# A float32 two-block network on one core: masks of the second block moved from TensorE to VectorE, tanh gates, and lighter VectorE work in the first block

## The chip, the cores and the metric

The kernel runs on one core of one Trainium2 chip. The metric is the device time of one execution in microseconds (us), a median over runs. The engines are named PE (TensorE), DVE (VectorE), ACT (ScalarE), POOL (GpSimd) and SP (SyncE, which here only starts transfers).

## The reference, cut to what matters

The first block is one layer: a projection into queries, keys, values, a convolution branch and a recurrent branch; three patterns of windowed attention; an output projection; a feed-forward part. The second block has two layers of latent attention (8 heads, 1040 tokens of which 16 are added in front) beside a pooling branch, each branch under a sigmoid gate.

```python
def conv_module(a, gate, dw_w, dw_b, ln_g, ln_b):
    u = a * jax.nn.sigmoid(gate)
    u = causal_depthwise_conv(u, dw_w, dw_b)            # 31 taps
    return jax.nn.silu(layernorm(u, ln_g, ln_b))
...
    u = causal_depthwise_conv(xr, cw, cb)               # 4 taps, then rg_lru
...
# second block, each of two layers
    y_pool = (pool_mix(u_pool, ...) * jax.nn.silu(z_pool)) @ pool_w_up[l]
    o_mla = mla(...)      # per head: softmax(mask(q k^T * scale)) v, causal
    y_mla = (o_mla * jax.nn.silu(z_mla)) @ mla_w_up[l]
    merged = jax.nn.sigmoid(g_pool) * y_pool + jax.nn.sigmoid(g_mla) * y_mla
    h_res = h_res + merged @ w_out[l]
```

## The kernel before

Channels lie on the partitions and tokens along the free axis. Every large product is made of three matmuls on a high and a low part of each operand (`mm3`, L125 to L127: high weight by high activation, high by low, low by high). `w()` (L109 to L119) brings a weight tile by a transfer that SP starts, copies its high part on ACT (L117) and makes the low part on DVE (L118). Results leave PSUM in 512-column pieces, or in pieces of 344 and 352 for the 1040 tokens. PSUM is split into 5 buffers with the tag mm and 3 with the tag ax. In SBUF there are pools u (30 tiles of a row block), s (10) and d (6). The engines run their instructions in a fixed order each; the framework sets that order when the kernel is built, from the order in which the code writes the work and from the priorities that it is given.

**First block.** While the projections into q, k and v run on PE, a list of background generators is stepped after every 512-column piece, by `pump` at the rate `RATE1` (60 before: 6.0 us of estimated DVE work to a piece). The generators are `conv_bg` (31 taps for each of two channel tiles, L429), `ln_bg` (layer norm after the convolution, L448 to L480) and three `lru_bg` (L486 to L526). `colsum` (L230) sums over partitions by matmuls against a column of ones, and `bcast` (L248) spreads the result. What is left of the background is run out by `hook` before attention starts. The drains of the projection are L396 (lx, lg) and L772 (q, k, v) on DVE.

**Second block.** `attn2` goes through the heads in steps (key tile j, query piece). `s_part` issues three matmuls into `st` (L1592 to L1594) and, where the step touches the diagonal, a fourth that adds the mask out of an identity times a mask table in bfloat16 (L1596). `evac` then takes the exponential on ACT (L1602), the high part `ph` on ACT or DVE (L1605, L1607) and the low part `pl` on DVE (L1608). `o_part` multiplies by the values (L1624 to L1626) three steps later (`LAG=3`). Between these matmuls stand those of the next head's preparation: `fp` (L1535) spreads norm factors over rows, `mx` (L1552, with the mask added in L1554) makes the scores once more to find each query's maximum (L1555 on DVE). Also between them stand the units of `fill`: the gate projections first, then the up-projection of the pooling branch (`mm<-th`), whose operand is read back from DRAM (`tr`, L1270 to L1273). `run` keeps back `keep` units of fill for the end of the last head: 2 for each of its columns before. After the last head the softmax sums go over DRAM (`rh`, L1473) and are spread by `rb` (L1490) before the up-projection of attention (`mm<-oh`) starts. The gates are taken by a sigmoid on ACT at L1282 (pooling) and L1407 (attention).

`fp` contracts over 57 rows (high part in rows 0 to 24, low part from row 32), `rb` over 40 (low part from row 32).

Of the kernel before, what the change touches and what calls it, by code (L numbers as in the profile page):

```python
# [11 lines left out]
F32R = mybir.dt.float32r  # L12
# [6 lines left out]
P = 128  # L19
# [27 lines left out]
def f(t):  # L47
    return t.bitcast(F32)


class B:
# [175 lines left out]
    def colsum(self, acc, tiles, nrows=P, pin=False):  # L227
        ps = self.axb("cs")
        for j, (c0, n) in enumerate(tiles):
            ins = self.nc.tensor.matmul(ps[:n, j:j + 1], acc[:nrows, c0:c0 + n], self.ones[:nrows, :], start=True, stop=True)  # L230
            if pin and j == 0:
                self.tc.keep_in_program_order(ins)
# [72 lines left out]
    def _block1(self):  # L305
# [140 lines left out]
        def ln_bg():  # L446
            sm = self.u("sm")
# [5 lines left out]
            mub = self.u("mub")  # L453
# [3 lines left out]
            q0, q1 = self.u("q"), self.u("q")  # L457
# [12 lines left out]
            rb = self.u("rb")  # L470
# [3 lines left out]
            for ct in range(2):  # L474
                a = cv[ct]
                nc.vector.tensor_tensor(a[:, :S], a[:, :S], rb[:, :S], op=OP.mult)
                sg = self.u("sg")
                nc.scalar.activation(sg[:, :S], a[:, :S], AF.Sigmoid, scale=col("lng", ct), bias=col("lnb", ct))
                nc.vector.tensor_scalar(a[:, :S], a[:, :S], col("lng", ct), col("lnb", ct), op0=OP.mult, op1=OP.add)
# [4 lines left out]
        def lru_bg(i):  # L484
            uu = self.u("uu")
            nc.vector.tensor_scalar(uu[:, :S], lx[i][:, :S], col("lw", 9 + i), col("lb", i), op0=OP.mult, op1=OP.add)  # L486
            yield 1.2
# [5 lines left out]
            r, ig = self.u("r"), self.u("ig")  # L493
# [36 lines left out]
        lx, lg = [], []  # L530
        for i in range(3):
# [8 lines left out]
            self.bg.append(lru_bg(i))  # L540
# [29 lines left out]
        def hook(stp):  # L570
            if stp == (0, 0, 0):
                self.flush()
                self.rate = 0
            if stp == (1, 0, 0):
                mix_in(5)
                mix_in(6)
                mix_in(7)
# [106 lines left out]
    def attn1(self, xh, xl, wk, win, scaled, hook):  # L684
# [7 lines left out]
        for hh in range(2):  # L692
            nc.vector.tensor_copy(bm[:, 3 * hh:3 * hh + 3, :], bmf[hh][:, :768].rearrange("p (a b) -> p a b", a=3))
# [127 lines left out]
        def s_part(g, j, b):  # L821
# [240 lines left out]
    def layer(self, l):  # L1062
# [190 lines left out]
        def fill():  # L1253
# [14 lines left out]
            for g in range(4):  # L1268
# [3 lines left out]
                nc.vector.tensor_copy(h[:, M0:], t[:, M0:])  # L1272
                nc.vector.tensor_tensor(lo[:, M0:], t[:, M0:], f(h[:, M0:]), op=OP.subtract)  # L1273
                th.append(h)
                tl.append(lo)
            for m in range(8):
# [5 lines left out]
                nc.scalar.activation(t[:, M0:], t[:, M0:], AF.Sigmoid)  # L1282
                y = mp[m] = self.u("mp")
                for c0, n in CM:
                    ps = self.mmb()
                    for k in range(4):
# [3 lines left out]
                        if k == 3:  # L1290
                            nc.vector.tensor_tensor(y[:, c0:c0 + n], ps[:, :n], t[:, c0:c0 + n], op=OP.mult)
# [32 lines left out]
        fr = self.ur("frh", (57, L2))  # L1324
        nc.gpsimd.memset(f(fr[0:57, :]), 0.0)

        def qstats():
# [8 lines left out]
            for g in range(3):  # L1336
# [7 lines left out]
                nc.vector.tensor_tensor(fr[32:57, c0:c0 + wd], ps[0:25, :wd], f(fr[0:25, c0:c0 + wd]), op=OP.subtract)  # L1344
# [56 lines left out]
        for m in range(8):  # L1401
# [5 lines left out]
            nc.scalar.activation(t[:, M0:], t[:, M0:], AF.Sigmoid)  # L1407
# [5 lines left out]
            def ev(ci, c0, n, ps, t=t, y=y, h=h, lo=lo):  # L1413
                nc.vector.tensor_tensor(t[:, c0:c0 + n], ps, t[:, c0:c0 + n], op=OP.mult)
# [44 lines left out]
    def rlgrp(self, l, h0, h1):  # L1459
# [11 lines left out]
        for q, t in ((0, rlh), (32, rll)):  # L1471
# [27 lines left out]
    def attn2(self, l, fr, fill):  # L1499
# [10 lines left out]
        self.rh = self.ur("rh", (40, L2))  # L1510
        nc.gpsimd.memset(f(self.rh[0:40, :]), 0.0)
# [394 lines left out]
```

## Time and profile before

| what | value |
|---|---|
| median of 3 runs | 2974.47 us (2971.53 to 2975.08) |
| the profiled execution's own time | 2971.57 us |
| its span | 2969.8 us |
| PE busy | 2893.7 us (97%) |
| DVE busy | 1707.3 us (57%) |
| ACT busy | 973.8 us (33%) |
| POOL busy | 33.7 us (1%) |
| mean granted TensorE clock | 0.984 |

Busy time is the time in which at least one instruction of an engine is under way. Matmuls overlap: a row of 512 columns is shown with 0.39 us, but such rows start 0.23 us apart. So a busy PE can still be a PE that does less than it could, and the distance from one start to the next is what a matmul costs. The chain of waits follows the work that ended last back from the end. A number in brackets behind a row of the timeline is the idle time just before the instruction, with the instruction or transfer that ended it.

### The profile page before, as it was taken

Reading aid. Unit: us, or ns where it says so; the run is one execution under the profiler, and the core shown is the slowest. Engines: PE = TensorE matmul, PEld = TensorE weight load, DVE = VectorE, ACT = ScalarE, POOL = GpSimd, SP = SyncE. Lnnn points to the kernel's source line nnn. Section 1 sums busy time; section 2 is a strip of 40 time slices with the busy share of each in tenths; the row PEclk is TensorE's granted clock in tenths of the full one; section 3 lists DMA queues with packets and bytes.
Section 4 is the critical chain, followed back from the end, with each engine's and each line's share of the span. In section 5 each row is a group of like instructions: output and inputs, shape, how many; then the busy total and the mean of one; then the engine's idle time right before and its main releaser. Section 6 shows DMA issues by size and latency. Waiting matters only on the chain.

```text
span 2969.8 us, 37159 instructions
## 1 busy us (share of the span) xinstructions
PE 2893.7 (97%) x14918; PEld 2442.2 (82%) x14918; DVE 1707.3 (57%) x2940; ACT 973.8 (33%) x1617; POOL 33.7 (1%) x101
## 2 busy tenths in 40 slices
PE   8979999999999999999999999989999999999999
PEld 6857788888888888899899998879978887777677
DVE  6986766544545546544665665564534665656562
ACT  4143432111111124433234343743432223433630
POOL 1000000000000000000000000000000000000000
PEclk9989999999999999999999999989999999999999
DMA  3111212111111111524223232532313323232542
GB/s 129 54 36 64 86 59 69 46 50 50 43 50 50 43 47 53 174 62 125 65 83 91 76 101 59 187 112 105 123 54 98 116 75 91 88 85 74 177 141 76
DMA packets 93520, 249.93 MB, mean 84 GB/s; under 512 B 29489, under 2 KB 30786, under 8 KB 93348
## 3 DMA queue, kind: packets, MB, share of 16 engines
q1 hardware_dynamic: 93348, 247.56, 26.3%
q8 instruction: 117, 1.92, 0.3%
q14 instruction: 55, 0.45, 0.0%
HBM read 182.86 MB, written 60.06 MB: 82 GB/s over the span
## 4 chain that ended last, share of the span: by engine, by line
PE 93%; DVE 4%; ACT 1%; DMA 1%; issue 0%; SPq 0%; POOL 0%; DVEq 0%; ACTq 0%; POOLq 0%
PE mm L125 27%; PE mm L127 26%; PE mm L126 26%; PE mx L1552 1%; PE st L1593 1%; PE st L1594 1%; PE st L1592 1%; PE ob L1624 1%; PE ob L1626 1%; PE ob L1625 1%; PE fp L1535 1%; PE cs L230 1%; PE mxp L720 0%; PE mx L1554 0%; PE st L1596 0%
## 5 line engine op out<-in xcount | busy, mean ns | idle before, releaser
L125 PE MATMUL mm<-xh,wh 128*128 128x512 f32 (+2 forms) x2352 | 879.0, 375 | 25.7 <-DVE kf L772 10.9
L127 PE MATMUL mm<-xh,wl 128*128 128x512 f32 (+2 forms) x2352 | 855.5, 364 | 0.2 <-POOL wl L118 0.2
L126 PE MATMUL mm<-xl,wh 128*128 128x512 f32 (+2 forms) x2352 | 854.3, 364 | 0.0
L125 PEld LDWEIGHTS mm<-xh,wh 128*128 128x128 f32 x2352 | 448.4, 191 | 91.1 <-DVE kf L772 12.5
L127 PEld LDWEIGHTS mm<-xh,wl 128*128 128x128 f32 x2352 | 445.6, 189 | 58.1 <-issue 0.7
L126 PEld LDWEIGHTS mm<-xl,wh 128*128 128x128 f32 x2352 | 447.2, 190 | 52.8 <-issue 0.9
L117 ACT ACTIVATE wh<-wr 128x1024 fp32r<-128x1024 f32 (+2 forms) x217 | 221.9, 1023 | 811.6 <-PE mm L126 627.4
L118 DVE TENSOR_TENSOR wl<-wr,wh 128x1024 fp32r<-128x1024 f32 (+2 forms) x215 | 253.3, 1178 | 122.2 <-ACT wh L117 121.4
L1602 ACT ACTIVATE p<-st 128x272 f32<-128x272 f32 (+8 forms) x256 | 106.1, 414 | 325.7 <-PE st L1596 179.1
L127 PE MATMUL mm<-fh,wl 128*128 128x512 f32 x512 | 201.5, 394 | 0.0
L126 PE MATMUL mm<-fl,wh 128*128 128x512 f32 x512 | 201.1, 393 | 0.0
L125 PE MATMUL mm<-fh,wh 128*128 128x512 f32 x512 | 201.1, 393 | 0.0
L1608 DVE TENSOR_TENSOR pl<-p,ph 128x272 fp32r<-128x272 f32 (+8 forms) x256 | 118.1, 462 | 143.5 <-ACT ph L1605 140.2
L655 DVE TENSOR_TENSOR x<-mm,x 128x512 f32<-128x512 f32 x208 | 142.3, 690 | 97.3 <-PE mm L127 96.9
L625 DVE SCALAR_TENSOR_TENSOR ft<-mm,zs 128x512 f32<-128x512 f32 x64 | 44.1, 691 | 166.3 <-PE mm L127 164.9
L1555 DVE TENSOR_REDUCE mxp<-mx 128x1 f32<-128x512 f32 (+9 forms) x232 | 116.6, 522 | 38.6 <-PE mx L1552 22.2
L126 PEld LDWEIGHTS mm<-fl,wh 128*128 128x128 f32 x512 | 96.2, 188 | 22.4
L125 PEld LDWEIGHTS mm<-fh,wh 128*128 128x128 f32 x512 | 96.1, 188 | 22.2
L127 PEld LDWEIGHTS mm<-fh,wl 128*128 128x128 f32 x512 | 96.1, 188 | 21.8
L127 PE MATMUL mm<-gh,wl 128*128 128x512 f32 (+2 forms) x320 | 112.2, 351 | 0.0
L126 PE MATMUL mm<-gl,wh 128*128 128x512 f32 (+2 forms) x320 | 112.2, 350 | 0.0
L125 PE MATMUL mm<-gh,wh 128*128 128x512 f32 (+2 forms) x320 | 111.9, 350 | 0.0
(437 smaller groups left out, 4600.7 us busy)
## 6 DMA issues: line engine op xcount, KB each, us to landing
wr<-in_w_in SPq DMA_DIRECT2D x91, 512.0 KB
wr<-in_w_up SPq DMA_DIRECT2D x32, 512.0 KB
wr<-in_w_down SPq DMA_DIRECT2D x26, 512.0 KB
wr<-in_wo SPq DMA_DIRECT2D x16, 512.0 KB
wr<-in_wq SPq DMA_DIRECT2D x12, 384.0 KB
hd<-hr SPq DMA_DIRECT2D x8, 520.0 KB
kd<-kn SPq DMA_DIRECT2D x8, 520.0 KB
kf<-kd SPq DMA_DIRECT2D x16, 260.0 KB
```

Of the source, the lines that this page charges most:

```text
L117: nc.scalar.activation(hi[:, :width], raw[:, :width], AF.Copy)
L118: self.loe.tensor_tensor(lo[:, :width], raw[:, :width], f(hi[:, :width]), op=OP.subtract)
L125: nc.tensor.matmul(ps, wh, xh, start=first and q == 0, stop=False)
L126: nc.tensor.matmul(ps, wh, xl, start=False, stop=False)
L127: nc.tensor.matmul(ps, wl, xh, start=False, stop=last and q == n - 1)
L230: ins = self.nc.tensor.matmul(ps[:n, j:j + 1], acc[:nrows, c0:c0 + n], self.ones[:nrows, :], start=True, stop=True)
L625: nc.vector.scalar_tensor_tensor(t, ps, 0.0, zs[:, c0:c0 + n], op0=OP.max, op1=OP.mult)
L655: nc.vector.tensor_tensor(x[:, c0:c0 + n], ps, x[:, c0:c0 + n], op=OP.add)
L1535: nc.tensor.matmul(ps[0:R, :n], self.esel[:, e, 0:R], fr[:, c0:c0 + n], start=True, stop=True)
L1555: nc.vector.tensor_reduce(mxp[:n, i, ci:ci + 1], ps[:n, :k1 - k0], axis=AX, op=OP.max)
L1602: nc.scalar.activation(p[:kn, :w], st[:kn, :w], AF.Exp, scale=SC)
L1608: nc.vector.tensor_tensor(pl[:kn, :w], p[:kn, :w], f(ph[:kn, :w]), op=OP.subtract)
```

## The change

In the first block, work with one tensor operand goes from DVE to ACT: the first tap of the convolutions, the last scale and shift of the layer norm, the copies of the queries for attention, two table copies. The two sums of the layer norm's tiles are dropped, and `colsum` adds both tiles in PSUM instead (it takes a list). Temporaries of `ln_bg` and `lru_bg` move to pool d. The rate falls from 6.0 to 4.4, and `hook` may go on pumping in the first pattern of attention (`LRA`).

In the second block, both mask matmuls go. The mask of `mx` is added in the instruction that takes the maximum (`tensor_tensor_reduce` with a table `mz`, which is the mask with 512 zero columns in front), and the mask of `st` is added in place on DVE ahead of the exponential. The sigmoid gates become tanh of half the argument, with the halves folded into `th` and `ep`. The low rows of `fp` and `rb` start at 64 rather than 32, so these contract over 89 and 72 rows. `keep` is doubled.

```diff
     def colsum(self, acc, tiles, nrows=P, pin=False):
...
+            accs = acc if isinstance(acc, list) else [acc]
+            for q, ac in enumerate(accs):
+                ins = self.nc.tensor.matmul(ps[:n, j:j + 1], ac[:nrows, c0:c0 + n], self.ones[:nrows, :],
+                                            start=q == 0, stop=q == len(accs) - 1)
...
-            nc.vector.tensor_scalar(a[:, :S], uc[ct][:, :S], col("cw", 2 * 30 + ct), col("cb", ct), op0=OP.mult, op1=OP.add)
-            yield 0.7
+            nc.scalar.activation(a[:, :S], uc[ct][:, :S], AF.Identity, scale=col("cw", 2 * 30 + ct), bias=col("cb", ct))
+            yield 0.1
...
-            nc.vector.tensor_tensor(sm[:, :S], cv[0][:, :S], cv[1][:, :S], op=OP.add)
             yield YD
-            cs = self.colsum(sm, self.T1, pin=PIN)
+            cs = self.colsum([cv[0], cv[1]], self.T1, pin=PIN)
...
-            nc.vector.tensor_scalar(uu[:, :S], lx[i][:, :S], col("lw", 9 + i), col("lb", i), op0=OP.mult, op1=OP.add)
+            nc.scalar.activation(uu[:, :S], lx[i][:, :S], AF.Identity, scale=col("lw", 9 + i), bias=col("lb", i))
...
             if stp == (0, 0, 0):
+                self.rate = 0
+                self.late = True
...
+            if stp[0] == 0:
+                self.pump(LRA)
...
-                nc.vector.tensor_copy(qzh[R, :], QH[g][R, :S])
-                nc.vector.tensor_copy(qzl[R, :], QL[g][R, :S])
+                nc.scalar.activation(qzh[R, :], f(QH[g][R, :S]), AF.Copy)
+                nc.scalar.activation(qzl[R, :], f(QL[g][R, :S]), AF.Copy)
...
-                nc.scalar.activation(t[:, M0:], t[:, M0:], AF.Sigmoid)
+                nc.scalar.activation(t[:, M0:], t[:, M0:], AF.Tanh, scale=0.5)
...
-                            nc.vector.tensor_tensor(y[:, c0:c0 + n], ps[:, :n], t[:, c0:c0 + n], op=OP.mult)
+                            nc.vector.scalar_tensor_tensor(y[:, c0:c0 + n], t[:, c0:c0 + n], 1.0, ps[:, :n], op0=OP.add, op1=OP.mult)
...
-        fr = self.ur("frh", (57, L2))
+        fr = self.ur("frh", (89, L2))
...
-        self.rh = self.ur("rh", (40, L2))
+        self.rh = self.ur("rh", (72, L2))
...
                     if has:
-                        nc.tensor.matmul(ps[:n, dg - k0:k1 - k0], self.idb[:n, :n], self.mk[:n, 1, dg - q0:k1 - q0], start=False, stop=True)
-                    nc.vector.tensor_reduce(mxp[:n, i, ci:ci + 1], ps[:n, :k1 - k0], axis=AX, op=OP.max)
+                        z0 = 512 + k0 - q0
+                        nc.vector.tensor_tensor_reduce(ps[:n, :k1 - k0], ps[:n, :k1 - k0], self.mz[:n, z0:z0 + k1 - k0], 1.0, -3.0e38,
+                                                       OP.add, OP.max, mxp[:n, i, ci:ci + 1])
+                    else:
+                        nc.vector.tensor_reduce(mxp[:n, i, ci:ci + 1], ps[:n, :k1 - k0], axis=AX, op=OP.max)
...
-            if diag:
-                mms.append(lambda: nc.tensor.matmul(st[:kn, 0:d1 - s0], self.idb[:kn, :kn], self.mk[:kn, 0, s0 - 128 * j:d1 - 128 * j],
-                                                    start=False, stop=True))
...
+                if diag:
+                    nc.vector.tensor_tensor(st[:kn, 0:d1 - s0], st[:kn, 0:d1 - s0], self.mk[:kn, 0, s0 - 128 * j:d1 - 128 * j], op=OP.add)
                 nc.scalar.activation(p[:kn, :w], st[:kn, :w], AF.Exp, scale=SC)
...
-            keep = 2 * len(CQ0) * 4
+            keep = 4 * len(CQ0) * 4
...
-_PARAMS = dict(PHD=5, PHA=4, LAG1=2, RATE1=60, LAG=3,
+_PARAMS = dict(PHD=5, PHA=4, LAG1=2, RATE1=44, LRA=4, LAG=3,
```

On PE 304 mask matmuls leave the order (152 into `mx`, 152 into `st`) and 16 matmuls of `cs` come. On ACT the loads of activation tables fall from 54 to 18. On DVE 152 of the maxima become pairs of instructions, and 152 additions come.

How a diagonal step reads on PE in layer 0 of the second block, before (`mx` scores for the next head, `mm` a gate projection, `st` scores of this head, `mk` the mask):

```order
L1552 MATMUL mx_12679<-kh_12454,qh_12452 128x128
L1554 LDWEIGHTS idb
L1554 MATMUL mx_12679<-mk,idb 128x128
L125 MATMUL mm_12620<-xh_7829,wh_12524 128x344
L126 MATMUL mm_12620<-xl_7830,wh_12524 128x344
L127 MATMUL mm_12620<-xh_7829,wl_12525 128x344
L1592 MATMUL st_12687<-qh_11878,kh_11880 128x256
L1593 MATMUL st_12687<-ql_11879,kh_11880 128x256
L1594 MATMUL st_12687<-qh_11878,kl_11881 128x256
L1596 LDWEIGHTS idb
L1596 MATMUL st_12687<-mk,idb 128x128
L125 MATMUL mm_12698<-xh_7403,wh_12524 128x344
```

The two masks and the loads of their identity are gone from PE. In such steps of the changed kernel DVE has, in layer 0 (`gt` a gate projection's drain, `pl` the low part of the probabilities, `ISA mx,mxp` the addition with maximum and `ISA mxp` its second instruction):

```order
L1275 TENSOR_TENSOR gt_13517<-mm_13636,zs 128x344
L1621 TENSOR_TENSOR pl_13700<-p_13698,ph_13699 128x384
L1566 ISA mx_13717,mxp_13631<-mx_13717,mz 128x512
L1566 ISA mxp_13631 128x1
L1645 TENSOR_TENSOR osb_13642<-osb_13642,zt_13643 64x384
L1569 TENSOR_REDUCE mxp_13631<-mx_13720 128x1
L1614 TENSOR_TENSOR st_13726<-st_13726,mk 128x128
L1566 ISA mx_13747,mxp_13631<-mx_13747,mz 128x128
L1566 ISA mxp_13631 128x1
L1621 TENSOR_TENSOR pl_13733<-p_13731,ph_13732 128x384
```

The addition to `st` stands behind whatever DVE has in its queue, and ACT's exponential of that step behind it.

The end of the last head of layer 0 on PE, before (`ob` values by probabilities, `rb` the spread of the softmax sums, `mm<-oh` the first matmul after it):

```order
L127 MATMUL mm_16014<-th_15224,wl_15910 128x344
L1624 MATMUL ob_15755<-ph_15836,vh_14772 65x272
L1625 MATMUL ob_15755<-ph_15836,vl_14773 65x272
L1626 MATMUL ob_15755<-pl_15837,vh_14772 65x272
L1624 MATMUL ob_15755<-ph_15861,vh_14772 65x144
L1625 MATMUL ob_15755<-ph_15861,vl_14773 65x144
L1626 MATMUL ob_15755<-pl_15862,vh_14772 65x144
L1624 MATMUL ob_15755<-ph_15885,vh_14772 65x16
L1625 MATMUL ob_15755<-ph_15885,vl_14773 65x16
L1626 MATMUL ob_15755<-pl_15886,vh_14772 65x16
L1490 MATMUL rb_16030<-rh_10269,ep 128x352
```

The same place after the change, from the last but one piece of `ob`:

```order
L1637 MATMUL ob_15598<-ph_15703,vh_14652 65x144
L1638 MATMUL ob_15598<-ph_15703,vl_14653 65x144
L1639 MATMUL ob_15598<-pl_15704,vh_14652 65x144
L125 MATMUL mm_15777<-th_15253,wh_15749 128x344
L126 MATMUL mm_15777<-tl_15254,wh_15749 128x344
L127 MATMUL mm_15777<-th_15253,wl_15750 128x344
L125 MATMUL mm_15777<-th_15259,wh_15749 128x344
L126 MATMUL mm_15777<-tl_15260,wh_15749 128x344
L127 MATMUL mm_15777<-th_15259,wl_15750 128x344
L1637 MATMUL ob_15598<-ph_15728,vh_14652 65x16
L1638 MATMUL ob_15598<-ph_15728,vl_14653 65x16
L1639 MATMUL ob_15598<-pl_15729,vh_14652 65x16
```

Matmuls of the pooling branch now stand between the pieces of `ob`, and another 126 of them between the last piece and `rb`; in layer 1 it is 72. Before there were none between.

In the first block, DVE's order around the first drain of the keys, before (`uu` and `ig` of the recurrent branch):

```order
L486 TENSOR_SCALAR uu_1091<-lx_842,cols 128x1024
L516 SCALAR_TENSOR_TENSOR uu_1018<-a_1067,ig_1024 128x1024
L490 SCALAR_TENSOR_TENSOR uu_1091<-lx_842,cols,uu_1091 128x1023
L779 TENSOR_TENSOR ql_1095<-qf_991,qh_1094 128x512 x2
L490 SCALAR_TENSOR_TENSOR uu_1091<-lx_842,cols,uu_1091 128x1022
L772 TENSOR_TENSOR kf_1106<-mm_1107,zs 128x512
```

And after the change (`cv` a tap of the convolution):

```order
L783 TENSOR_TENSOR qf_979<-mm_1010,zs 128x512
L118 TENSOR_TENSOR wl_1129<-wr_1126,wh_1128 128x1024
L432 SCALAR_TENSOR_TENSOR cv_503<-uc_408,cols,cv_503 128x1008
L790 TENSOR_TENSOR ql_1041<-qf_979,qh_1040 128x512
L432 SCALAR_TENSOR_TENSOR cv_503<-uc_408,cols,cv_503 128x1007
L783 TENSOR_TENSOR kf_1052<-mm_1053,zs 128x512
```

The drain of the keys stands 37 places earlier in DVE's order (171 in place of 208), and taps of the convolution stand around it where the recurrent branch stood before. All of the background still stands ahead of the first step of attention.

## Rows read from the trace of the kernel before

**Rows 1.** The page: busy time of each engine, and the chain by engine.

```profile
PE 2893.7 (97%) x14918; PEld 2442.2 (82%) x14918; DVE 1707.3 (57%) x2940; ACT 973.8 (33%) x1617; POOL 33.7 (1%) x101
PE 93%; DVE 4%; ACT 1%; DMA 1%; issue 0%; SPq 0%; POOL 0%; DVEq 0%; ACTq 0%; POOLq 0%
```

**Rows 2.** Stretches: length, then busy us (instructions) by engine, clock, DMA.

```profile
100.00:150.00 50.00, 50.00 (x217) 40.55 (x217) 49.84 (x49) 5.31 (x5) 0.00 (x0) 1.00 0.18 58
180.00:200.00 20.00, 8.74 (x20) 4.42 (x19) 17.66 (x18) 10.61 (x13) 0.00 (x0) 0.53 0.00 0
1438.00:1893.00 455.00, 446.86 (x2858) 410.21 (x2857) 283.26 (x579) 174.79 (x385) 6.73 (x27) 0.99 0.31 92
```

**Rows 3.** Timeline of PE, start and duration: with a mask, and without.

```profile
1602.34 0.23 PE L1554 MATMUL mx<-mk,idb 128*128 128x128 bf16 x1
...
1602.62 0.32 PE L126 MATMUL mm<-xl,wh 128*128 128x344 f32 x1
...
1610.31 0.32 PE L125 MATMUL mm<-xh,wh 128*128 128x352 f32 x1
1610.47 0.32 PE L126 MATMUL mm<-xl,wh 128*128 128x352 f32 x1
```

**Rows 4.** The line of one kind of mask matmul.

```profile
L1596 PE MATMUL st<-mk,idb x152: 171/231/233, 1527.8 to 2812.3; 128*128 128x128 bf16 x112, 16*16 16x16 bf16 x16, 128*128 128x112 bf16 x16, 128*128 128x16 bf16 x8
```

**Rows 5.** PE timeline around matmuls over 40 and 70 rows; the lines' counts.

```profile
1890.29 0.33 PE L1626 MATMUL ob<-pl,vh 128*65 128x384 f32 x1
1890.55 0.42 PE L1490 MATMUL rb<-rh,ep 40*128 40x352 f32 x1
1890.90 0.43 PE L125 MATMUL mm<-th,wh 128*128 128x352 f32 x1
1891.17 0.33 PE L126 MATMUL mm<-tl,wh 128*128 128x352 f32 x1
...
312.06 0.28 PE L847 MATMUL st<-sha,selr 70*128 70x256 f32 x1
312.19 0.28 PE L849 MATMUL st<-mk,idb 128*128 128x256 bf16 x1
...
L1535 PE MATMUL fp<-frh,esel x88: 279/393/472, 1439.1 to 2720.2; 57*97 57x344 f32 x32, 57*97 57x352 f32 x16, 57*96 57x384 f32 x16, 57*96 57x512 f32 x16
L1490 PE MATMUL rb<-rh,ep x20: 418/485/630, 1881.4 to 2830.4; 40*128 40x344 f32 x8, 40*128 40x512 f32 x8, 40*128 40x352 f32 x4
```

**Rows 6.** Waits of PE (total, times, longest); table loads ahead of the exponential.

```profile
PE rb L1490 <- DMA rh<-rll: 9.4, 2, 6.8
PE mm L125 <- DVE th L1272: 7.6, 2, 4.8
PE ob L1624 <- ACT ph L1605: 6.8, 3, 3.7
...
L1602 ACT ACT_TABLE_LOAD x20 | 25.7, 1283 | 0.3
```

**Rows 7.** PE's timeline right after the waits that end layer 0.

```profile
1949.34 0.49 PE L127 MATMUL mm<-oh,wl 128*128 128x352 f32 x1
1949.63 0.49 PE L125 MATMUL mm<-oh,wh 128*128 128x344 f32 x1
```

**Rows 8.** First block: a wait of PE, and operations of one tensor operand.

```profile
194.62 0.79 PE L125 MATMUL mm<-xh,wh 128*128 128x512 f32 x1 [10.88 <-DVE kf L772]
144.00 0.81 DVE L486 TENSOR_SCALAR uu<-lx,cols 128x1024 f32<-128x1024 f32 x1
L460 ACT ACTIVATE q<-cv 128x1024 f32<-128x1024 f32 x2 | 2.1, 1059 | 1.9 <-DVE cv L459 1.7
```

**Rows 9.** Second block, DVE's timeline: a long subtraction, a 128x128 one, a maximum.

```profile
1590.73 1.22 DVE L118 TENSOR_TENSOR wl<-wr,wh 128x1024 fp32r<-128x1024 f32 x1
1598.93 0.29 DVE L1608 TENSOR_TENSOR pl<-p,ph 128x128 fp32r<-128x128 f32 x1 [0.70 <-ACT ph L1605]
1602.60 0.56 DVE L1555 TENSOR_REDUCE mxp<-mx 128x1 f32<-128x384 f32 x1 [0.38 <-PE mx L1554]
```

More of the change, by code (lines that the diff above doesn't have):

```diff
@@ L229, in colsum @@
         for j, (c0, n) in enumerate(tiles):
-            ins = self.nc.tensor.matmul(ps[:n, j:j + 1], acc[:nrows, c0:c0 + n], self.ones[:nrows, :], start=True, stop=True)
-            if pin and j == 0:
-                self.tc.keep_in_program_order(ins)
+            accs = acc if isinstance(acc, list) else [acc]
+            for q, ac in enumerate(accs):
+                ins = self.nc.tensor.matmul(ps[:n, j:j + 1], ac[:nrows, c0:c0 + n], self.ones[:nrows, :],
+                                            start=q == 0, stop=q == len(accs) - 1)
+                if pin and j == 0 and q == 0:
+                    self.tc.keep_in_program_order(ins)
         t = self.tiny("csb")
@@ L476, in ln_bg @@
                 nc.vector.tensor_tensor(a[:, :S], a[:, :S], rb[:, :S], op=OP.mult)
-                sg = self.u("sg")
+                sg = (q0, q1)[ct]
                 nc.scalar.activation(sg[:, :S], a[:, :S], AF.Sigmoid, scale=col("lng", ct), bias=col("lnb", ct))
-                nc.vector.tensor_scalar(a[:, :S], a[:, :S], col("lng", ct), col("lnb", ct), op0=OP.mult, op1=OP.add)
+                nc.scalar.activation(a[:, :S], a[:, :S], AF.Identity, scale=col("lng", ct), bias=col("lnb", ct))
                 nc.vector.tensor_tensor(a[:, :S], a[:, :S], sg[:, :S], op=OP.mult)
@@ L492, in lru_bg @@
                 yield 1.2
-            r, ig = self.u("r"), self.u("ig")
+            lt = self.u if self.late else self.d
+            self.held.append(i)
+            r, ig, a = lt("r"), lt("ig"), lt("a")
             yield YD
@@ L530, in _block1 @@
         lx, lg = [], []
+        self.late, self.held = False, []
+        lrus = []
         for i in range(3):
@@ L571, in hook @@
             if stp == (0, 0, 0):
+                self.rate = 0
+                self.late = True
+                while self.bg and (self.bg[0] not in lrus or lrus.index(self.bg[0]) in self.held):
+                    for _ in self.bg.pop(0):
+                        pass
+            if stp[0] == 0:
+                self.pump(LRA)
+            if stp == (1, 0, 0):
                 self.flush()
-                self.rate = 0
-            if stp == (1, 0, 0):
                 mix_in(5)
@@ L1406, in layer @@
             nc.sync.dma_start(t[:, M0:], self.gmd[l][m][:, M0:])
-            nc.scalar.activation(t[:, M0:], t[:, M0:], AF.Sigmoid)
+            nc.scalar.activation(t[:, M0:], t[:, M0:], AF.Tanh, scale=0.5)
             h, lo = self.ur("gh"), self.ur("gl")
@@ L1470, in rlgrp @@
         rh = self.rh
-        for q, t in ((0, rlh), (32, rll)):
+        for q, t in ((0, rlh), (64, rll)):
             for h in range(h0, h1):
@@ L1551, in prep @@
                     has = dg < k1
-                    nc.tensor.matmul(ps[:n, :k1 - k0], qh[0:96, q0:q0 + n], kh[0:96, k0:k1], start=True, stop=not has)
+                    nc.tensor.matmul(ps[:n, :k1 - k0], qh[0:96, q0:q0 + n], kh[0:96, k0:k1], start=True, stop=True)
                     if has:
-                        nc.tensor.matmul(ps[:n, dg - k0:k1 - k0], self.idb[:n, :n], self.mk[:n, 1, dg - q0:k1 - q0], start=False, stop=True)
-                    nc.vector.tensor_reduce(mxp[:n, i, ci:ci + 1], ps[:n, :k1 - k0], axis=AX, op=OP.max)
+                        z0 = 512 + k0 - q0
[3 more added lines that the diff above has]
+                        nc.vector.tensor_reduce(mxp[:n, i, ci:ci + 1], ps[:n, :k1 - k0], axis=AX, op=OP.max)
                     yield
@@ L1593, in s_part @@
                    lambda: nc.tensor.matmul(st[:kn, :w], kh[0:96, ksl], ql[0:96, s0:c1], start=False, stop=False),
-                   lambda: nc.tensor.matmul(st[:kn, :w], kl[0:96, ksl], qh[0:96, s0:c1], start=False, stop=not diag)]
-            if diag:
-                mms.append(lambda: nc.tensor.matmul(st[:kn, 0:d1 - s0], self.idb[:kn, :kn], self.mk[:kn, 0, s0 - 128 * j:d1 - 128 * j],
-                                                    start=False, stop=True))
+                   lambda: nc.tensor.matmul(st[:kn, :w], kl[0:96, ksl], qh[0:96, s0:c1], start=False, stop=True)]
             def evac():
```

62 lines of the change are left out of this document (32 added, 30 removed).

## The prediction

> **What bounds the kernel now.** I read the page first: PE is busy in 97% of the span and 93% of the chain is PE [rows 1]. So the time falls only where PE has less to do, does it at a shorter distance from start to start, or waits less. A busy PE is not a PE at its best, so I then read its timeline by the distance from one start to the next. Rows of 352 columns start 0.16 us apart; around a mask matmul and around the matmuls over few rows the distance is longer [rows 3, 5]. Third, the stretches: in the first block DVE is the full engine (49.84 of 50 us) while PE keeps up, and later a stretch follows in which PE works 8.74 of 20 us at a clock of 0.53 [rows 2]. In the second block PE works 446.86 of 455 us and DVE 283.26. Last, the list of waits: three of its lines belong to the ends of the two layers' attention [rows 6].
>
> **The masks.** They remove 152 matmuls from `mx` and 152 from `st` (the line of one kind is in [rows 4]; the other has the same count). The price of one is not its 0.23 us row but the longer distance. From the mask's start at 1602.34 to the second matmul after it at 1602.62 are 0.28 us. Without a mask the first of the three starts 0.16 before the second. So the mask costs 0.12 [rows 3]. Over all places I find a middle of 0.13, with 0.24 for the few masks of 16 columns. 304 by 0.13 is **40 us**, all on PE's path; the ends are 30 (0.10) and 49 (0.16).
>
> **57 and 40 rows become 89 and 72.** Around one `rb` over 40 rows the starts are 0.26, 0.35 and 0.27 apart, 0.88 together. Neighbours of 384 and 352 columns would need 0.17, 0.16 and 0.16. So 0.39 is lost for one episode [rows 5]. `fp` comes in pairs (88 rows in about 44 episodes, 0.38 each), `rb` in 17 episodes: 61 by 0.39 is **24 us**. A matmul over 70 rows starts a successor 0.13 later, as any of its width, and loses nothing [rows 5]; 72 and 89 are above that. I take the whole 24; the lower end is 0, if the row count is not the cause.
> The Trainium skill, page "TensorEngine Tiling (Array Packing)", section "Key Properties", says that a change of the tiling mode drains TensorE, and it lists modes of 64 rows and less. The 40-row loss and the 70-row absence of one agree with that; by the page too the 24 us would go. It is why the rival below gets a small chance.
>
> **The ends of the layers.** In layer 0, PE waits three times for `ph`, 6.8 us, and then 6.8 for the last sums to come back [rows 6]. ACT is late, since each gate by sigmoid between two exponentials brings two table loads of 1.28 us; 20 loads stand ahead of exponentials [rows 6]. With tanh the loads of ACT fall from 54 to 18, and the matmuls of `th` stand between the pieces of `ob`. Another 126 stand between the last `ob` and `rb`: 126 by 0.16 is 20 us, more than the 6.8 us that the transfers need. Both waits go: 13.6. Afterwards PE runs at half clock: starts 0.29 apart instead of 0.16 [rows 7], over 16 matmuls, 2.1. Together **16 us**; the low end is 6.8, if the transfers still come last. In layer 1 the other part of the 9.4 for `rb` goes, 2.6, with about 0.9 of slow clock behind it: **3.5**; 72 matmuls of `th` (0.23 each, 17 us) cover it. The wait for the first `th` in both layers, 7.6 [rows 6], hangs on a round trip through DRAM and a cast that stays, on ACT now. It may gain 0 to 4, as no `rh` transfers are queued just ahead of it in layer 1; I take **2**.
>
> **First block.** Ahead of attention DVE loses 7 scale-and-add operations of 0.81 us, two table copies (1.1 together) and two sums (1.2 each): 9.2 us. The drain of the keys moves up by 37 places, past the recurrent branch, so the 10.88 us wait [rows 8] has no cause there any more. With its half clock the hole is some 13 us [rows 2]. But the work passed is not gone: the layer norm and the recurrent branch are now ahead of the drains of the last q and v pieces, and in that order I find a place where all 5 mm buffers are taken and PE waits some 7 us. PE also gets 16 more matmuls of `cs`, an estimate of 0.23 each between the 0.13 and 0.35 of [rows 5]: 3.6. The low bound is 0, the high one 20. I take 8, near 9.2 - 3.6 + 2 for the clock. The 12 copies of queries in the first attention leave DVE, which ends short waits of 0.7 there: 2. Together **10 us**.
>
> **What DVE pays.** 152 maxima get an addition with an extra short instruction, 152 steps an addition of up to 128 columns. The nearest rows: 0.56 for a maximum of 384, 0.29 for a 128x128 operation [rows 9]. The first is not in the trace: between +0.1 us (same pass, an extra read) and +0.7 (a second pass); I take 0.2. 152 by (0.2 + 0.3) is 76 us, 38 for each layer. In layer 0's stretch DVE comes to 283 + 38 of some 420 us, 76%; the values are used three steps after the scores, and a step is some 2.5 us. So the cover is about 7 us for a chain of addition, exponential, high and low part of some 4. I charge **5 us**, 0 to 15: where a 1.22 us subtraction [rows 9] and a maximum stand ahead, some steps will come late.
>
> **Sum.** 40 + 24 + 16 + 3.5 + 2 + 10 - 5 = 90.5. The profiled execution took 2971.57, which gives 2881; its time is 2.9 below the median of 2974.47, so the median comes to **2884**.
>
> **Rivals.** (a) *The row count is not the cause*: 89 rows pay as 57 did. 2884 + 24 = 2908. For it: 57 and 40 are the only such forms here, and 89 is none of the counts seen. Against it: 70.
> (b) *The wait is moved at the end of layer 0*: `th` matmuls wait for gates or drains on DVE, and PE again reaches `rb` before the sums. 16 + 3.5 do not come: 2904. Against it: 20 us of matmuls.
> (c) *ACT's share makes the first block no faster.* An operation of one operand over 1024 columns takes 1.06 on ACT and 0.81 on DVE [rows 8]. 25 such moves (7 scales, 12 copies, casts and tables) by 0.25 lengthen the chains by 6, the 10 are lost, and the time is 2884 + 10 + 6 = 2900. Against it: ACT is busy 5.31 of 50 us where DVE is full [rows 2].
> The Trainium skill, page "ScalarE: Activation LUTs", section "Rules for kernel authors", says that adds and multiplies belong on VectorE and not on ScalarE. The rows agree on the single operation (0.81 against 1.06); by the rule (c) is what comes.
> (d) *Slower: the diagonal step is paced by DVE.* The exponential waits for an addition that stands in DVE's queue. If half of a 1.22 us subtraction and its own 0.29 go onto PE's path at each of 152 steps, that is 0.9 by 152 = 137 us, in place of the 5: 2884 + 132 = 3016. It turns into a loss from (90.5 + 5) / 152 = 0.63 us for each step. Against it: three steps of cover, DVE at 76%.
>
> **How the numbers follow.** Forecast 0.62, (a) 0.13, (b) 0.08, (c) 0.10, (d) 0.05, and 0.02 that gains and losses cancel within 0.2%, about what a measurement can tell from no change. Faster 0.93, same 0.02, slower 0.05. The forecast's own ends, with the masks at 30 or 49, the first block at 0 or 20 and DVE at 0 or 15, reach some 2860 to 2905. To 2915 (a), (b) and (c) are inside, one at a time. Range 2860 to 2915.
>
> **What would show it.** Right: `mm` starts 0.16 apart around former masks and behind `fp`; no wait for `rh` at `rb`; no table loads between gates and exponentials; DVE 75 to 80% busy in the attention of layer 0. Wrong: waits of PE at `ob` for `pl` or `ph` in the middle of heads, or at `st` for an ax buffer (d); distances of 0.35 behind an 89-row `fp` (a); a new wait of more than 10 us ahead of 308 us (c).

## The result

| kernel | median | ratio to before, 95% interval |
|---|---|---|
| before | 2973.47 us (2971.53 to 2975.08, 4 runs) | |
| changed | 2937.13 us (2935.75 to 2939.89, 4 runs) | 0.9879 (0.9862 to 0.9896) |

36 us faster, where 90 were forecast and 2915 was the upper end of the range. The direction was right, the size was not. The page of the changed kernel, busy time of each engine and the chain:

```profile
PE 2862.6 (97%) x14646; PEld 2454.6 (84%) x14646; DVE 1720.8 (59%) x3214; ACT 958.9 (33%) x1610; POOL 34.3 (1%) x102
PE 91%; DVE 4%; ACT 2%; DMA 2%; issue 1%; SPq 0%; POOL 0%; DVEq 0%; ACTq 0%; POOLq 0%
```

PE lost 31 us of busy time against [rows 1] and no other engine became the bound. But the share of PE in the chain fell from 93 to 91%, and of transfers it rose from 1 to 2%. In PE's list of waits (total, times, longest), `zc` is new, and `qf`, `qh` and `kh` stood at 0.5, 1.0 and 0.3 us before:

```profile
PE bc L251 <- DVE zc L1059: 13.2, 1, 13.2
PE mm L125 <- DVE qf L783: 7.6, 1, 7.6
PE mx L1563 <- ACT qh L1548: 6.9, 7, 1.5
PE mm L125 <- ACT wh L328: 6.0, 1, 6.0
PE mt L1578 <- DVE mx L1572: 5.2, 2, 4.3
PE mm L125 <- DVE sg L399: 4.8, 1, 4.8
PE mxp L731 <- ACT kh L789: 4.3, 2, 3.5
...
PE mm L125 <- ACT th L1283: 3.1, 2, 2.8
```

The lines of [rows 6] on `rb` and `ob` are gone, `th` fell from 7.6 to 3.1, and the wait of [rows 8] for `kf` is 0.8. In their place come `zc`, `qf`, `qh` and `kh`, 32 us together. To see where, I cut the traces at the first matmul of each stage (us from one cut to the next):

| stage, from the first matmul of ... | before | changed | forecast of the difference (the prediction's terms, split by stage) |
|---|---|---|---|
| start to first block's attention (`st<-qzh`) | 304.6 | 315.1 | -8 |
| its attention to the feed-forward | 176.7 | 178.9 | -2 |
| feed-forward | 677.0 | 675.1 | 0 |
| to `mm<-ckh` (start of the second block) | 44.4 | 59.9 | 0 |
| layer 0, `st<-qh` to `mm<-oh` | 421.3 | 386.2 | -48 |
| layer 1, `st<-qh` to `mm<-oh` | 400.2 | 379.4 | -33 |

The two layers brought 56 us of some 80. The first block lost 12.7 (10.5 and 2.2) where it was to gain 10, and 15.5 us came in at a place that the prediction does not name. The three stretches that the table leaves out differ by at most 1.5 us.

### The profile page after: what moved, and what is told of

Same layout as the page of the kernel before. It is cut to its first block, busy times and chain, and to the rows that moved or that the text cites. A ratio compares the mean times of both kernels' runs of the same rounds, so it can differ in the third digit from the quotient of the medians.

```text
span 2937.8 us, 36780 instructions
## 1 busy us (share of the span) xinstructions
PE 2862.6 (97%) x14646; PEld 2454.6 (84%) x14646; DVE 1720.8 (59%) x3214; ACT 958.9 (33%) x1610; POOL 34.3 (1%) x102
## 4 chain that ended last, share of the span: by engine, by line
PE 91%; DVE 4%; ACT 2%; DMA 2%; issue 1%; SPq 0%; POOL 0%; DVEq 0%; ACTq 0%; POOLq 0%
PE mm L125 26%; PE mm L127 26%; PE mm L126 26%; PE mx L1563 1%; PE ob L1637 1%; PE ob L1639 1%; PE ob L1638 1%; PE st L1607 1%; PE st L1608 1%; PE st L1606 1%; DMA ef<-in_esel 1%; PE mxp L731 1%; PE cs L232 1%; PE fp L1546 0%; PE mxp L733 0%
## 5 line engine op out<-in xcount | busy, mean ns | idle before, releaser
L125 PE MATMUL mm<-xh,wh 128*128 128x512 f32 (+2 forms) x2352 | 867.7, 370 | 22.3 <-DVE qf L783 7.6
L1618 ACT ACTIVATE ph<-p 128x272 fp32r<-128x272 f32 (+8 forms) x206 | 92.6, 449 | 11.6 <-PE ob L1638 4.2
```

The costliest lines, as they stand in the source:

```text
L125: nc.tensor.matmul(ps, wh, xh, start=first and q == 0, stop=False)
L1618: nc.scalar.activation(ph[:kn, :w], p[:kn, :w], AF.Copy)
```

## The experiments

All medians but one are of four runs, with runs of the kernel before beside them (2972.1 to 2973.1); the changed kernel is 2937.13. Where a run starts from the changed kernel, "less" and "more" are against that; where it starts from the kernel before, the text says so.

**Two of the losses, and the head starts.** The wait at `zc` follows VectorE back to the table `esel`, whose casts wait for their transfers. DVE's timeline of the kernel before:

```profile
1167.51 0.56 DVE L1722 CAST esel<-ef 57x776 fp32r<-57x776 f32 x1 [3.32 <-DMA ef<-in_esel]
1169.71 0.56 DVE L1725 CAST esel<-ef 57x776 fp32r<-57x776 f32 x1 [1.65 <-DMA ef<-in_esel]
```

and of the changed kernel, with one microsecond ahead of the first cast (the last two numbers are the busy share of the 16 DMA engines and the transfers' rate in GB/s):

```profile
1186.46 0.56 DVE L1735 CAST esel<-ef 89x776 fp32r<-89x776 f32 x1 [11.60 <-DMA ef<-in_esel]
1197.50 0.56 DVE L1738 CAST esel<-ef 89x776 fp32r<-89x776 f32 x1 [10.48 <-DMA ef<-in_esel]
...
1176.00:1177.00 1.00, 1.00 (x8) 1.00 (x8) 0.00 (x0) 0.00 (x0) 0.00 (x0) 1.00 0.06 25
```

From one cast to the next, 276 KB in 11.0 us, where 177 KB took 2.2. Everything of the second block's first norm that runs on VectorE is queued behind these casts, `zc` at the end of it.

```diff
-        ef = self.u("ef", (89, 1024))
+        ef = self.u("ef", (96, 1024))      # esel padded in DRAM as well
...
-  self.esel[:, e, 0:R]
+  self.esel[0:89, e, 0:R]
```

> The changed kernel with the table esel padded from 89 to 96 rows in DRAM and in its transfer; the matmul still contracts over 89 rows. Theory (the 89-row transfer is carried at 25 GB/s, a third of the 75 to 80 GB/s of the 57-row one, and holds up VectorE): the two loads land within some 5 us, the wait of 13.2 us at bc<-zc goes, and the time falls by 13 to 16 us, to about 2922 us. Rival (the transfer is slow because of what else is in flight there, or because of its larger size): the wait stays above 8 us and the time falls by less than 5 us.

Measured: 2920.38 us, ratio 0.9818 (0.9803 to 0.9833), 16.8 less than the changed kernel. The wait at `zc` is gone. DVE's timeline:

```profile
1174.07 0.56 DVE L1735 CAST esel<-ef 96x776 fp32r<-96x776 f32 x1 [1.88 <-DMA ef<-in_esel]
1175.08 0.56 DVE L1738 CAST esel<-ef 96x776 fp32r<-96x776 f32 x1 [0.45 <-DMA ef<-in_esel]
```

A larger transfer at the same place is ten times as fast, so neither its size nor what else is in flight there is the cause.

```diff
 (first block as in the kernel before: conv_bg, ln_bg, lru_bg, hook, pools, table copies)
-RATE1=44
+RATE1=60
```

> The changed kernel with the first block's background as it was before (VectorE's scale-and-adds, one summed tile for each column sum, pool u, rate 6.0, all of the background ahead of attention); the query copies stay on ScalarE. Theory (the first block's part of the change loses time): attention starts at about 305 us instead of 315, and the time falls by 8 to 12 us, to about 2927 us. Rival (the 10 us come from the start of the kernel or from the run): the time stays within 3 us of 2937.

Measured: 2926.24 us, 0.9846 (0.9829 to 0.9862), 10.9 less. Attention starts at 303.7. The 10.88 us wait for `kf` is back, and the kernel is still faster: the changed first block is a loss of 11 us although it removes that wait. Against what the expectation says, this edit also puts the query copies back on VectorE. Its attention takes 176.6 us; kernels with the copies on ScalarE take 176.1 to 178.9, so at most some 2 of the 11 us can be theirs.

```diff
-            keep = 4 * len(CQ0) * 4
+            keep = 2 * len(CQ0) * 4
```

> The changed kernel with keep at 2 as before, so the heads have their old share of fill matmuls, and 54 (layer 0) and 30 (layer 1) matmuls instead of 126 and 78 stay between the last ob and the last rb. Theory (thinner fill at the start of a head uncovers the chain fp, kf, kh to mx): the waits of mx for qh fall from 6.9 us in 7 to under 2 us, and the time falls by 4 to 10 us. Rival (VectorE's longer queue alone makes qh late): the waits of mx for qh stay above 5 us and the time changes by less than 3 us, or grows by up to 5 us as the ends of the layers are less covered.

Measured: 2928.96 us, 0.985 (0.9836 to 0.9865), 8.2 less. The waits of `mx` for `qh` fall from 6.9 to 3.9, where the theory said under 2, and the wait for `th` grows from 3.1 to 7.0. The stages of layers 0 and 1 shorten by 5.2 and 2.7 us, the stage behind layer 0 grows by 1.5, so keep itself is worth some 6. The two layers' attention in the changed kernel and then here (length, busy time of each engine; the third number from the end is the granted clock of TensorE as a share of 2.4 GHz):

```profile
1554.10:1940.30 386.20, 380.11 (x2468) 364.57 (x2468) 261.96 (x663) 173.23 (x390) 2.41 (x26) 0.98 0.35 107
2421.00:2800.30 379.30, 371.26 (x1780) 295.32 (x1780) 245.02 (x581) 160.47 (x314) 1.56 (x17) 0.98 0.35 107
...
1547.00:1927.90 380.90, 375.49 (x2467) 360.58 (x2466) 262.03 (x663) 175.11 (x392) 2.39 (x26) 1.00 0.36 109
2410.30:2787.10 376.80, 368.63 (x1781) 292.36 (x1781) 245.79 (x581) 162.98 (x316) 1.55 (x17) 0.99 0.36 109
```

PE is idle for about as long (length less busy time: 14.1 us, here 13.6). What differs is the clock; an estimate from the clock's records in both traces puts it at some 8 us. The profiled execution is 13.4 us shorter, as its first block, the same program, took 7 us less in this profile (below). What keep does at a head's start can be read on PE. In the changed kernel:

```profile
2469.80 0.26 PE L1608 MATMUL st<-qh,kl 96*128 96x16 f32 x1
2471.02 0.34 PE L1563 MATMUL mx<-kh,qh 96*128 96x144 f32 x1 [0.97 <-ACT qh L1548]
2471.20 0.69 PE L125 MATMUL mm<-xh,wh 128*128 128x512 f32 x1
2471.68 0.63 PE L126 MATMUL mm<-xl,wh 128*128 128x512 f32 x1
2472.10 0.63 PE L127 MATMUL mm<-xh,wl 128*128 128x512 f32 x1
```

At the same head's start before:

```profile
2484.48 0.48 PE L125 MATMUL mm<-xh,wh 128*128 128x512 f32 x1
2484.79 0.39 PE L126 MATMUL mm<-xl,wh 128*128 128x512 f32 x1
2485.02 0.23 PE L1552 MATMUL mx<-kh,qh 96*128 96x144 f32 x1
```

Before, matmuls of fill stand between the last `fp` and the first `mx` and cover the chain over DVE and ACT. With more fill kept back there are none; PE idles 0.97 us and then works at half clock (0.42 us from start to start of the last two rows, where 0.23 is usual; granted clock 0.50 from 2472 to 2474 us).

**The parts alone, in the kernel before.**

```diff
-        fr = self.ur("frh", (57, L2))      # and rh 40 rows
+        fr = self.ur("frh", (89, L2))      # and rh 72 rows, esel moved as 96 rows
```

> The kernel before with fp over 89 and rb over 72 rows alone (the table's transfer padded to 96 rows). Theory (the row count is the cause of the 0.38 us for each of some 62 episodes): the time falls by 20 to 25 us against the kernel before, to about 2951 us. Rival (part of that was cover for waits elsewhere): it falls by less than 15 us.

Measured: 2955.74 us, 0.9943 (0.9928 to 0.9958): 17.4 less than before, between the two theories. The row count is the cause: only it and the table's transfer were changed, the two layers' attention shortens by 9.8 and 8.0 us, and in the changed kernel a `fp` over 89 rows stands among its neighbours without any loss,

```profile
1600.38 0.23 PE L1639 MATMUL ob<-pl,vh 128*65 128x144 f32 x1
1600.45 0.34 PE L1546 MATMUL fp<-frh,esel 89*97 89x344 f32 x1
1600.63 0.32 PE L125 MATMUL mm<-xh,wh 128*128 128x344 f32 x1
1600.79 0.32 PE L126 MATMUL mm<-xl,wh 128*128 128x344 f32 x1
```

0.18 and 0.16 to the next start, where [rows 5] has 0.35 and 0.27. Over all episodes (runs of such matmuls among others) the middle loss of `fp` fell from 0.37 to 0.02.

```diff
-                        nc.tensor.matmul(ps[:n, dg - k0:k1 - k0], self.idb[:n, :n], self.mk[...], start=False, stop=True)
+                        nc.vector.tensor_tensor_reduce(...)      # and the mask of st by an addition
```

> The kernel before with both masks on VectorE and nothing else changed. Theory (each mask matmul costs 0.13 us on TensorE, and VectorE's extra 76 us are hidden except at the heads' starts): the time falls by 30 to 40 us against the kernel before, to about 2938 us; waits of mx for qh at 2 to 5 us. Rival (VectorE's queue gives a good part back): it falls by 10 to 25 us, with waits of PE for VectorE's or ScalarE's work of over 10 us more than before in the two layers' attention.

Measured: 2956.5 us, 0.9947 (0.9931 to 0.9964): 16.2 less than before: the rival. Layer 0 gained 12.9 us and layer 1 only 4.0, and PE's waits grew where a layer ends:

```profile
PE rb L1490 <- DMA rh<-rll: 14.9, 2, 8.1
...
PE ob L1626 <- ACT ph L1607: 8.3, 5, 4.6
```

against 9.4 and 6.8 in [rows 6]. PE comes earlier to a place that waits for ScalarE and a transfer. In layer 1 PE's idle time grows from 7.8 to 16.5 us, and the granted clock falls from 0.99 to 0.98.

```diff
-            nc.scalar.activation(t[:, M0:], t[:, M0:], AF.Sigmoid)
+            nc.scalar.activation(t[:, M0:], t[:, M0:], AF.Tanh, scale=0.5)
```

> The kernel before with the tanh gates alone (halves folded into th and ep, casts of th on ScalarE), keep at 2. Theory (table loads make ScalarE late at the end of layer 0, which is worth the three waits of ob for ph, 6.8 us; the wait of rb for the sums needs more matmuls behind the last ob and stays): the time falls by 5 to 9 us against the kernel before. Rival (the gates alone give the whole end of layer 0, waits of rb too): it falls by 13 to 18 us.

Measured: 2953.94 us, 0.9935 (0.992 to 0.9949): 19.0 less than before, a little above the rival's range. My theory was too narrow. With keep still at 2, 54 matmuls of `th` now stand behind the last `ob` of layer 0, where none stood; that they do so because ScalarE delivers earlier is argued and not shown. Both kinds of wait go. In the profile layer 0 shortens by 15.7 us. Layer 1 does not (400.7 for 400.2): its wait at `rb` goes, but the clock falls from 0.99 to 0.98. Behind the `rb` of layer 0 no clock is lost: 15 us in which PE is 14.14 busy at full clock, with the three `rb` at their start.

```profile
1935.05 0.74 PE L1490 MATMUL rb<-rh,ep 40*128 40x352 f32 x3
...
1935.00:1950.00 15.00, 14.14 (x86) 13.59 (x86) 10.99 (x23) 7.20 (x12) 0.00 (x0) 1.00 0.40 143
```

**What in the first block costs 11 us.**

```diff
+            sm = self.d("sm")
+            nc.vector.tensor_tensor(sm[:, :S], cv[0][:, :S], cv[1][:, :S], op=OP.add)
-            cs = self.colsum([cv[0], cv[1]], self.T1, pin=PIN)
+            cs = self.colsum(sm, self.T1, pin=PIN)      # the second sum likewise
```

> The changed kernel with the two sums of the layer norm's tiles back on VectorE, so each of the two column sums of the first block is 16 short matmul rows again and not 32. Theory (the doubled run of one-column matmuls costs 1.8 us twice, and the clock falls to half behind it for about 9 us of matmuls): the clock stays full between 180 and 200 us, and the time falls by 6 to 9 us. Rival (the order of VectorE's work is the loss of the first block): the time changes by less than 3 us.

Measured: 2928.16 us, 0.985 (0.9836 to 0.9865), 9.0 less. The time came as said, the reason did not: the clock between 180 and 200 us was 0.60, lower than the 0.74 of the changed kernel. Each run of `cs` rows shrinks from some 3.7 to 1.84 us, 3.7 together; what the other 5 are stays open.

```diff
-RATE1=44
+RATE1=60
```

> The changed kernel with the background's rate at 6.0 as before, and everything else of the first block changed. Theory (the loss lies in the column sums): the time stays within 4 us of 2937. Rival (the lower rate leaves layer norm and recurrent branch to the last projections): the waits for qf and kh fall from 12 us to under 5 us, and the time falls by 6 to 11 us.

Measured: 2923.22 us, 0.9833 (0.9818 to 0.9847), 13.9 less: the rival. It is even a little more than the rival said. Of the waits for `qf` and `kh` nothing is left above 0.5 us; there are 3.3 for `kf` and 2.6 for `cv` instead. The stretches 240 to 260 and 260 to 280 in the changed kernel,

```profile
240.00:260.00 20.00, 17.38 (x47) 9.69 (x48) 7.34 (x18) 4.48 (x8) 0.77 (x1) 0.57 0.06 24
260.00:280.00 20.00, 12.41 (x44) 9.16 (x43) 13.02 (x14) 16.84 (x18) 2.07 (x3) 0.83 0.13 53
```

and with the old rate:

```profile
240.00:260.00 20.00, 20.00 (x88) 13.47 (x87) 15.35 (x28) 11.98 (x15) 2.90 (x4) 1.00 0.21 80
260.00:280.00 20.00, 20.00 (x82) 14.75 (x81) 14.61 (x19) 3.08 (x5) 0.00 (x0) 0.83 0.24 86
```

At the low rate VectorE is 7.34 of 20 us busy in the first stretch, so it is not short of time. The layer norm and the recurrent branch come late and then stand, in chains over PE, DVE and ACT, ahead of the drains of the last projections. The clock itself varies here from run to run. Five kernels have the same order of instructions in this block. In four of them (the changed one, and those with the 96-row table, with 95 and 93 rows, and with the mask of `st` on TensorE) the clock falls during or just behind the first run of `cs` rows and is 0.66 to 0.74 between 180 and 200 us. With keep at 2 it is 1.00 there, and attention starts at 308.0 where the others have 313.3 to 315.1. In all five PE is shown busy throughout that stretch. Why the clock differs is open.

**Together.**

> The changed kernel with the 96-row table, the old first block and keep at 2 together. Theory (the three losses are separate places): the three gains add up, 17 + 11 + 8 = 36 us, to about 2901 us. Rival (the gains overlap, as one wait takes the place of another): 2910 us or more.

Measured, for the 96-row table with the old first block and keep at 2: 2910.16 us, 0.979 (0.9775 to 0.9804). 27 of 36: the rival's side, just. The old first block brings its own 306 us to attention.

```diff
 96-row table, single sums, RATE1=60, keep = 2 * ... (next run: keep = 3 * ...)
```

> The changed kernel with the 96-row table, single sums, rate 6.0 and keep at 2. Theory (the three losses are apart, and rate and sums each cost in the first block): attention starts at 298 to 303 us, the two layers' attention takes about 381 and 377 us, and the time is 2895 to 2902 us. Rival (the rate's gain and the sums' are the same 10 us): attention starts at 301 us or later and the time is 2903 to 2910 us.

> As the run before with keep at 3. Theory (fill is shared between the heads' starts and the layers' ends, and both are short): within 3 us of keep at 2, with the wait for th smaller and the waits of mx for qh larger. Rival (one of the two places decides): 4 us or more apart.

Measured: 2901.86 us, 0.9761 (0.9747 to 0.9776), with attention from 299.7 and 382.4 and 376.7 us for the two layers: at the upper end of the theory's range. With keep at 3, 2900.15 us, 0.9754 (0.974 to 0.9769). Keep at 3 shrinks the wait for `th` from 6.5 to 1.1 and lets that for `qh` grow from 3.9 to 4.8; the times are the same within 2 us, as the theory said. This is the fastest version, called the mended kernel below: 73 us under the kernel before, 37 under the changed one.

**What the masks are worth.**

```diff
 changed kernel:
+                mms.append(lambda: nc.tensor.matmul(st[:kn, 0:d1 - s0], self.idb[:kn, :kn], self.mk[...], start=False, stop=True))
-                    nc.vector.tensor_tensor(st[:kn, 0:d1 - s0], ...)
```

> The changed kernel with the mask of st back on TensorE, that of mx stays on VectorE. Theory (VectorE's addition ahead of the exponential costs little, the 152 matmuls cost 0.11 to 0.13 us each): the time rises by 10 to 18 us. Rival (VectorE's queue is what the missing gain went to): the time stays within 4 us of 2937 or falls, with the waits of st and mx for p and qh gone.

Measured: 2945.45 us, 0.991 (0.9894 to 0.9927): 8.3 more, between the two theories; 8.3 is 152 by 0.055.

```diff
 mended kernel with keep at 3: both masks on TensorE again
```

> The run with keep at 3 and all mends, with both masks back on TensorE. Theory (with the layers' ends covered, a mask is worth its gross price of about 0.11 us less some waits): 22 to 32 us slower than with the masks on VectorE, about 2927 us. Rival (VectorE's queue gives half back wherever the ends are): 10 to 18 us slower, about 2914 us.

Measured: 2921.55 us, 0.9829 (0.9811 to 0.9846): 21.4 more, just under the theory's range. In this kernel's trace a mask costs 0.13 as before, 39.5 together; with the masks on VectorE the layers shorten by 13.0 and 9.9. So some 17 to 18 us are given back even with the layers' ends covered. The two layers' attention with the masks on TensorE, and then on VectorE:

```profile
1520.30:1914.50 394.20, 389.34 (x2604) 364.90 (x2603) 245.31 (x528) 173.45 (x391) 2.35 (x26) 1.00 0.34 105
2395.90:2783.20 387.30, 383.78 (x1931) 295.91 (x1931) 225.64 (x431) 160.47 (x315) 1.55 (x17) 1.00 0.33 105
...
1518.60:1899.70 381.10, 376.10 (x2468) 361.96 (x2467) 261.60 (x663) 172.95 (x391) 2.42 (x26) 0.99 0.35 109
2381.10:2758.40 377.30, 371.61 (x1780) 294.69 (x1780) 244.34 (x581) 161.43 (x315) 1.55 (x17) 0.99 0.34 108
```

With the masks on VectorE PE is idle for 10.7 us in place of 8.4, and the granted clock is 0.99 in place of 1.00; an estimate from the clock's records puts the slower clock at some 7 us. The waits of `mx` for `qh` are nearly the same in both, 4.8 and 4.3 us, so they are not what the masks cost. No single wait carries the loss, and 7 to 8 us of it are not placed.

**Why 89 rows are slow.**

```diff
-        nc.sync.dma_start(ef[:, :776], self.i["esel"][:, 0:776])
+        nc.sync.dma_start(ef[0:95, :776], self.i["esel"][0:95, 0:776])
...
+        nc.sync.dma_start(ef[0:93, :776], self.i["esel"][0:93, 776:1552])
```

> The changed kernel with a 96-row table in DRAM of which the first transfer of esel takes 95 rows and the second 93. Theory (the rows are dealt out in equal parts, in as many parts up to 16 as divide the row count: 57 = 3 x 19 gave 75 to 83 GB/s, 89 is a prime and gave 25, 96 gave over 300): the stretch of the first runs at about 5 x 25 = 125 GB/s and takes 2 to 3 us, the second at 3 x 25 = 75 GB/s and takes 3.5 to 4 us. Rival (only an exact share for all 16 is fast, everything else falls to one engine): 25 GB/s and 11 us each. Second rival (size alone): both over 250 GB/s.

One run: 2921.74 us. The second transfer landed 4.05 us behind the first, at 74 GB/s. The last two numbers of the lines with a stretch are again the share of the 16 DMA engines and the rate; after the lines of this run stand one with 57 rows (the kernel before) and one with 96:

```profile
1175.07 0.56 DVE L1735 CAST esel<-ef 95x776 fp32r<-95x776 f32 x1 [2.46 <-DMA ef<-in_esel]
1179.12 0.56 DVE L1738 CAST esel<-ef 93x776 fp32r<-93x776 f32 x1 [3.50 <-DMA ef<-in_esel]
...
1176.00:1177.00 1.00, 1.00 (x8) 1.00 (x7) 0.00 (x0) 0.00 (x0) 0.00 (x0) 1.00 0.19 74
...
1166.00:1167.00 1.00, 1.00 (x8) 1.00 (x7) 0.00 (x0) 0.00 (x0) 0.00 (x0) 1.00 0.19 78
...
1173.00:1174.00 1.00, 1.00 (x8) 1.00 (x8) 0.00 (x0) 0.00 (x0) 0.00 (x0) 1.00 1.02 260
```

93 is 3 x 31 and moves at 74 GB/s, 57 is 3 x 19 and moved at 74 to 81, 89 is a prime and moved at 25: the theory of divisors holds. The shares agree: 0.19 of 16 engines is three, the 0.06 of the 89 rows is one, and with 96 rows all 16 are busy. The table's rows are packets of 3104 bytes, and in the trace of this run those of the 95 rows (5 x 19) stand five at a time. The Trainium skill states it, page "DMA: Bandwidth & Descriptors", section "Why a DMA increments its semaphore by 16 and not by 1": a transfer runs on the largest number of engines, up to 16, that divides the slowest dimension of both its sides. All five row counts seen here agree.

## Why the prediction was wrong, step by step

- **Row counts**: right in mechanism (0.37 to 0.02 for an episode), 17.4 us alone for 24. Where the difference went is not shown.
- **Masks**: the gross price was right (39.5 for 40). The term that was mis-sized is what DVE pays: 5 us with 15 as the upper end, measured 18 with the layers' ends covered and about 24 without (40 less the 16.2). The prices of the instructions were right: the addition with maximum takes 0.69 for 512 columns, as the maximum alone, with 0.14 for its second instruction, and the addition to `st` 0.30. DVE is 70% busy in layer 0, where I had 76 (first line; the others are of the whole kernel):

```profile
1570.00:1850.00 280.00, 275.95 (x1810) 263.50 (x1810) 194.87 (x509) 121.60 (x288) 1.73 (x19) 0.99 0.31 89
L1566 DVE CUSTOM_DVE_ANT_0 mx<-mx,mz 128x512 f32<-128x512 f32 x32 | 22.1, 691 | 3.6 <-PE mx L1563 3.6
L1566 DVE DVE_READ_ACCUMULATOR2_ANT mxp<- 128x1 f32 x144 | 19.7, 137 | 0.0
L1614 DVE TENSOR_TENSOR st<-st,mk 128x128 f32<-128x128 f32 x112 | 33.1, 298 | 31.9 <-PE st L1608 31.5
```

  I argued from that share and from three steps of cover for `ob`. What I left out is that many small delays of PE add up, and that a slower clock follows some of them: 2.3 us of waits and some 7 of clock in the pair of kernels with both masks here or there. The rest of the 18 is not placed. Rival (d) named the queue but put 0.9 us on each of the 152 steps; 18 us are 0.12.
- **Ends of the layers**: right in place and nearly in size. The gates alone give 19.0 for 21.5, in the profile all of it in layer 0. One edit, the gates, removes both waits there; I gave half of it to the order with more fill behind the last `ob`. Doubling keep was not needed for it and cost some 6 us at the heads' starts, which I did not price: I listed what fill covers at the end and not what it had covered where it was taken from. What keep did bring is the wait for the first `th`: 3.1 us in the changed kernel, 6.5 to 7.9 with keep at 2. (In layer 1, 78 matmuls of `th` stand ahead of `rb`, and 18 stood there before; I had written 72 and none.)
- **First block**: the step that failed by sign, 10 gained in the forecast and 11 lost. I counted the work that leaves DVE and gave the lower rate no price. But the lower rate moves the background later, and the time to look at was the end of the stage. The wait of some 7 us that I had found there in the order is not in my sum of 9.2 - 3.6 + 2; it was measured as 7.6, with 3.5 more for `kh` and a slow clock beside them. With the old rate and single sums the block gains 5 to 9 us (attention from 299.7 and 296.0 for 304.6), which is what the forecast said of the moved work. One term of it was right by luck: 32 matmuls of `cs` came and not 16 (PE's count falls by 272, which is 304 less 32), at 0.11 us each and not 0.23, so 3.6 us came out either way.
- **The table's transfer**: not in the prediction at all. I priced 89 rows on PE and not the transfer that brings them: 16.8 us. When a shape is edited, every use of it has to be priced.

The forecast was 90.5 us. The mended kernel has 73 of them. Of the 17.5 that it lacks, VectorE's term is 13 (18 for 5). The row counts and the gates alone gave 7 and 2.5 less than forecast, and the first block's gain of 5 to 9 is 1 to 5 short; that is more than is lacking, so terms measured alone do not simply add. The same holds for the 37 us from the mended to the changed kernel. One by one the mends gave 16.8 (table), 13.9 (rate), 9.0 (single sums) and 8.2 us (keep at 2), 48 in all. Table, rate, sums and keep at 2 together gave 35, so parts of them are the same time; which parts is not shown.

The forecast's own ends, taken together, reach 2914 and not 2905; the range up to 2915 held them, and the result lies 22 us above it.

None of the rivals is the result. (c) had the right block and the wrong mechanism: undoing the rate alone, with the work still on ScalarE, gave 13.9 us, so it is the order and not the price of an operation on ScalarE.

## What to carry to other kernels

When a dimension is changed to suit one engine, price the transfer that fills it too, and give it a row count with a large divisor up to 16. Fill that is kept for one gap is taken from another, so list both. Work moved to an engine that is 70% busy can still cost the critical engine something at many places: ask for each chain what stands beside it on the critical engine, and not how busy the helper is. And read the granted clock beside the waits; here it cost more than they did.

## What the runs showed that was not expected

A 276 KB load of 89 rows ran at 25 GB/s on one DMA engine, one of 93 at 74 on three, and one of 96 landed 1.0 us behind the one before it. Matmuls over 72 and 89 rows pay 0.02 us an episode where 40 and 57 rows paid 0.37 to 0.39. TensorE's clock differed between runs of one order of instructions in a stretch in which the engine is shown busy throughout (0.66 to 0.74 in four, 1.00 in one, between 180 and 200 us); the one with 1.00 came to attention 5 to 7 us earlier. And between two kernels that idle alike in the second block's attention, the clock alone made some 8 us.
